# A hybrid attention and mLSTM layer: terms of the later modulation sums begin with the fifth iteration of the attention loop in place of the first

## The chip, the cores and the metric

The kernel runs on one core of one Trainium2 chip. The metric is the device time of one execution in microseconds (us). Engines are named as in the profile: PE is TensorE, DVE VectorE, ACT ScalarE, POOL GpSimd, and SP the SyncE queue that issues nearly all DMAs.

## The reference

One layer on 1024 latent tokens and 256 context tokens, all of width 1024, in float32. The parts that matter here:

```python
mod = jax.nn.silu(c) @ w_mod[l] + b_mod[l]                     # 1024 -> 6 * 1024
sh1, sc1, g1, sh2, sc2, g2 = jnp.split(mod, 6, axis=-1)
h = modulate(rms_norm(x, norm1_w[l]), sh1, sc1)
aq, ak, av, mq, mk, mv, mo, mg, ga, gm = split_in_proj(h @ w_in[l])
att = windowed_gqa(q, k, v, k_ctx, v_ctx, attn_sink[l])        # 16 heads, 4 groups, window 128
ml = mlstm_readout(ht, mo, ml_norm_w[l])                       # two mLSTM scans
y = merge_branches(att, ml, ga, gm, w_branch_att[l], w_branch_ml[l], w_out[l])
x_mid = x + g1[:, None, :] * y
x = x_mid + g2[:, None, :] * conv_ffn(modulate(rms_norm(x_mid, norm2_w[l]), sh2, sc2), ...)
```

The first two sixths of `mod` (sh1, sc1) are needed before anything else. The other four (g1, sh2, sc2, g2) are needed only behind the two mixers. They are "the later modulation sums" of the title.

## The kernel before, in words

Every float32 operand of a large product is split into a high part of fewer bits and the rest (`split_from`, L49: a copy on ACT, L44, and a subtraction on DVE), and three products are made of the pairs (`mm3`, L96 to L98). Weights come by DMA through two raw buffers (`w1r`, L71) and are split likewise (ACT `w1h`, DVE `w1l`, L74).

The stages follow each other: a startup with the context's keys and values, attention, the mLSTM (it begins with gate mathematics and projections `kv`), the merge, the feed-forward part.

Attention runs over 4 head groups g and 8 blocks b of 128 tokens, 32 pairs in all, as a pipeline of 37 iterations n. Iteration n makes the projection of pair n (`proj`), the transposed query and key of pair n - 1 (`stacks`), the scores and the softmax of pair n - 3 (`scores`), and the products with the values of pair n - 4 (`pv`). The softmax's mask step is L625 on DVE, its exponential L629 on ACT, its scaling L638 on POOL. The block of scores `s` has one PSUM buffer for the four heads of a pair, so the scores of a head wait for the mask step of the head before it. Between these, PE is given products of a later need (`filler`, L711: the sigmoid gates' projection, weights `fr`, results `g`, stored from `fo`), 24 an iteration.

Beside that the loop makes the later modulation sums. A sum has 512 columns of `w_mod`. Its k-th term is a 128 x 512 piece of the weights times a column of silu(c), added to the running sum `macc` on DVE. The first term is `tensor_scalar` (L219) and the seven others `scalar_tensor_tensor` (L221). `mod_load` (L206) brings the next piece into `wmb`, of which there is one buffer, as there is of `macc`. Behind the eighth term `mod_row` sums over the partitions on PE (L232, `ms`), adds the bias on DVE (L234), and for the second sum stores g1. Six sums, 48 terms, belong to attention; two more are made at the end of the kernel.

The order on each engine is not the order of the code. A list scheduler under the kernel places instructions by its own model of when they are ready, code order deciding between those that are; it may move an instruction far ahead of code that stands before it. Each engine then runs its list strictly in that order, and waits on semaphores.

Of the kernel before, what the change touches and what calls it, by code (L numbers as in the profile page):

```python
# [105 lines left out]
def layer_kernel(ctx: ExitStack, tc: tile.TileContext, A: dict, out: bass.AP, dbg=None):  # L106
# [58 lines left out]
    with ExitStack() as st:  # L165
        at = attention_setup(E, st)
        stage_startup(E, at)
        if "hT" in dbg:
            for k in range(KT):
                nc.sync.dma_start(dbg["hT"][0, k * P : (k + 1) * P], hH[k].bitcast(F32))  # L170
                nc.sync.dma_start(dbg["hT"][1, k * P : (k + 1) * P], hL[k].bitcast(F32))
        if dbg.get("stop") != "hT":
            stage_attention(E, st, at)
# [35 lines left out]
def mod_product(E, pool, n, last):  # L209


    nc, (i, k) = E.nc, divmod(n, KT)
    q, o = i // 2, i % 2 * 4
    if k == 0:
        E.macc = pool.tile([P, 512], F32, tag="macc", name=f"macc{i}", bufs=1)
        E.maccs[i] = E.macc
    w = E.wmod
    if k == 0:
        nc.vector.tensor_scalar(E.macc, w, E.sil[:, 0:1], None, op0=ALU.mult)  # L219
    else:  # L220
        nc.vector.scalar_tensor_tensor(E.macc, w, E.sil[:, k : k + 1], E.macc, op0=ALU.mult, op1=ALU.add)  # L221
    if k == KT - 1:
        mod_row(E, pool, i)
    if n + 1 < last:
        mod_load(E, pool, n + 1)
# [295 lines left out]
def stage_attention(E, st, at):  # L521
# [55 lines left out]
    def stacks(g, b):  # L577
        n = f"{g}_{b}"
        qf, ss = S1.pop((g, b))
        kf = wp.tile([P, 2, HD], F32, tag="kf", name=f"kf{n}", bufs=2)  # L580
        nc.vector.tensor_scalar(kf, qf[:, None, 256:320].to_broadcast([P, 2, HD]), ss[:, 4:5], None, op0=ALU.mult)


        pt = tp_tile(f"qt{n}")
        for i in range(2):
            nc.tensor.transpose(pt[:, i * P : (i + 1) * P], qf[:, i * P : (i + 1) * P], ident)
        nc.tensor.transpose(pt[:, 256:384], kf.rearrange("p r d -> p (r d)"), ident)
        QT = wp.tile([P, 512], F32R, tag="QT", name=f"QT{n}", bufs=3)
        Q4 = QT.rearrange("p (i r t) -> p r i t", i=2, r=2)
        pq = pt[:, 0:256].rearrange("p (i t) -> p i t", i=2)  # L590
        halves = slice(0, HD), slice(HD, P)
        for r in range(2):
            hi, lo = halves[r], halves[1 - r]
            copy_act(nc, Q4[hi, r], pq[hi])
        ts = sl(b * P, P)
        copy_act(nc, G[g]["KA"][:, ts], pt[:, 256:384])
        for r in range(2):
            hi, lo = halves[r], halves[1 - r]
            nc.vector.tensor_tensor(Q4[lo, r], pq[hi], Q4[hi, r].bitcast(F32), op=ALU.subtract)
        nc.vector.tensor_tensor(G[g]["KB"][:, ts], pt[:, 256:384], G[g]["KA"][:, ts].bitcast(F32), op=ALU.subtract)  # L600
        S2[(g, b)] = (QT, ss)
# [39 lines left out]
    def pv(g, b):  # L641
        n = f"{g}_{b}"
        Ps, b0, b1 = S3.pop((g, b))
        nk = b1 - b0 + NCB
        po = mm_tile(f"po{n}")
        parts = []

        def values(kb, prior=None):
            ph, plo = parts[kb]
            v = G[g]["V"][:, b0 + kb] if kb < b1 - b0 else Vc[:, kb - (b1 - b0), g]  # L650
            with behind(prior):
                nc.tensor.matmul(po, v, ph, start=kb == 0, stop=False)
                nc.tensor.matmul(po, v, plo, start=False, stop=kb == nk - 1)

        for kb in range(nk):
            pt = tp_tile(f"pt{n}_{kb}")
            for h in range(4):
                turned = nc.tensor.transpose(pt[:, h * P : (h + 1) * P], Ps[h][:, kb * P : (kb + 1) * P], ident)  # L658
            ph = pp.tile([P, 512], F32R, tag="ph", name=f"ph{n}_{kb}", bufs=3)
            plo = pp.tile([P, 512], F32R, tag="pl", name=f"pl{n}_{kb}", bufs=3)  # L660
            split_from(nc, ph, plo, pt)
            parts.append((ph, plo))
            if kb >= 2:
                values(kb - 2)
        values(nk - 2)
        values(nk - 1, FILL.products(6))
        o2 = wp.tile([HD, 512], F32, tag="o2", name=f"o2{n}", bufs=1)
        copy_act(nc, o2, po[HD:P])
        nc.vector.tensor_tensor(o2, po[0:HD], o2, op=ALU.add)
        nc.sync.dma_start(  # L670
            attT_d[g * 256 : (g + 1) * 256, b * P : (b + 1) * P].rearrange("(h d) t -> d h t", d=HD),
            o2.rearrange("d (h t) -> d h t", h=4),
        )
# [21 lines left out]
    def filler(n):  # L695
        c, t = n // 2, n % 2
        if t == 0:
            fh = fp.tile([P, KT, P], F32R, tag="fh", name=f"fh{c}")
            fl = fp.tile([P, KT, P], F32R, tag="fl", name=f"fl{c}")
            for i in range(2):  # L700
                raw = wts.rp.tile([P, 2, 400], F32, tag="raw", name=f"fr{c}_{i}").rearrange("p a b -> p (a b)")
                raw = raw[:, :512].rearrange("p (k c) -> p k c", c=P)
                nc.sync.dma_start(raw, A["w_g"][c][:, 4 * i : 4 * i + 4, :])
                split_from(nc, fh[:, 4 * i : 4 * i + 4], fl[:, 4 * i : 4 * i + 4], raw)
            FW[c] = [(fh[:, k], fl[:, k]) for k in range(KT)]
        ps = E.fl_tile(f"g{c}_{t}")
        ts = sl(t * 512, 512)
        todo = [(w, x[:, ts]) for (wh, wl), (xh, xl) in zip(FW[c], hT) for w, x in ((wh, xh), (wh, xl), (wl, xh))]

        def one(i, w, x):  # L710
            return lambda: nc.tensor.matmul(ps, w, x, start=i == 0, stop=i == len(todo) - 1)  # L711

        FILL.todo = [one(i, w, x) for i, (w, x) in enumerate(todo)]
        FILL.tile = c, t, ps

    def filled():
        if not FILL.todo and FILL.tile is None:
            return
        FILL.products(len(FILL.todo))
        c, t, ps = FILL.tile  # L720
        FILL.tile = None
        o = fp.tile([P, 512], F32, tag="fo", name=f"fo{c}_{t}", bufs=1)
        copy_act(nc, o, ps)
        dst = (E.sga_d, E.sgm_d)[c // 8]
        nc.sync.dma_start(dst[(c % 8) * P : (c % 8 + 1) * P, t * 512 : (t + 1) * 512], o)
# [5 lines left out]
    done = 0  # L731
    mod_load(E, dp, 0)
    for n in range(N + 5):
        if n % 2 and done < 48:
            mod_product(E, dp, done, 48)
            done += 1
        if n < N:
            proj(*seq[n])
        if 0 <= n - 1 < N:
            stacks(*seq[n - 1])  # L740
        if n not in SKIPS and n < N + len(SKIPS):
            filler(n - sum(s < n for s in SKIPS))
        if 0 <= n - 3 < N:
            scores(*seq[n - 3])
        if 0 <= n - 4 < N:
            pv(*seq[n - 4])
        filled()
        if done < 48:
            mod_product(E, dp, done, 48)
            done += 1  # L750

# [1281 lines left out]
```

## Time and profile before

| what | value |
|---|---|
| time, median of 3 runs | 1908.57 us (1906.63 to 1910.79) |
| time of the profiled execution | 1906.98 us |
| span of the profiled execution, first to last instruction | 1904.9 us |
| PE busy | 1878.7 us, 99% of the span |
| DVE busy | 1439.1 us, 76% |
| ACT busy | 994.3 us, 52% |
| POOL busy | 310.6 us, 16% |
| granted PE clock, mean | 0.999 |

The lines of a profile read so: start in us from the beginning of the span, duration, engine, line of the kernel, operation, what it writes <- what it reads, and in brackets how long the engine stood before it and what ended that. Buffer numbers are left out of the names. A line can be a helper's, as L44 and L49 are, so tiles tell more than lines.

### The profile page before, as it was taken

Reading aid. Unit: us, or ns where it says so; the run is one execution under the profiler, and the core shown is the slowest. Engines: PE = TensorE matmul, PEld = TensorE weight load, DVE = VectorE, ACT = ScalarE, POOL = GpSimd, SP = SyncE. Lnnn points to the kernel's source line nnn. Section 1 sums busy time; section 2 is a strip of 40 time slices with the busy share of each in tenths; the row PEclk is TensorE's granted clock in tenths of the full one; section 3 lists DMA queues with packets and bytes.
Section 4 is the critical chain, followed back from the end, with each engine's and each line's share of the span. In section 5 each row is a group of like instructions: output and inputs, shape, how many; then the busy total and the mean of one; then the engine's idle time right before and its main releaser. Section 6 shows DMA issues by size and latency. Waiting matters only on the chain.

```text
span 1904.9 us, 28762 instructions
## 1 busy us (share of the span) xinstructions
PE 1878.7 (99%) x10021; PEld 1629.9 (86%) x10021; DVE 1439.1 (76%) x2904; ACT 994.3 (52%) x1974; POOL 310.6 (16%) x524
## 2 busy tenths in 40 slices
PE   7999999999999999999999999999999999999999
PEld 4888888988888899999998887888888888888887
DVE  3967778877677766667577878679888889897565
ACT  4735656556556445454446664276444444465441
POOL 1223424333332231212020012000000000000000
PEclk9999999999999999999999999999999999999999
DMA  9542222222122423334318963613355444489841
GB/s 365 190 135 65 68 71 74 92 67 79 59 64 84 136 85 127 126 126 166 136 54 309 378 252 136 229 67 111 143 195 194 185 163 171 171 321 352 293 166 67
DMA packets 139569, 298.53 MB, mean 157 GB/s; under 512 B 15504, under 2 KB 39968, under 8 KB 136608
## 3 DMA queue, kind: packets, MB, share of 16 engines
q1 hardware_dynamic: 125024, 270.48, 40.8%
q10 hardware_dynamic: 14400, 26.22, 4.0%
q8 instruction: 79, 1.29, 0.3%
q14 instruction: 66, 0.54, 0.1%
HBM read 220.55 MB, written 76.10 MB: 156 GB/s over the span
## 4 chain that ended last, share of the span: by engine, by line
PE 87%; DVE 6%; DMA 2%; ACT 2%; POOL 2%; issue 1%; POOLq 0%; SPq 0%; DVEq 0%; ACTq 0%
PE g L711 9%; PE pa L1610 4%; PE pa L1612 4%; PE pa L1611 4%; PE pt L658 3%; PE yb L1612 2%; PE yb L1611 2%; PE yb L1610 2%; PE kv L96 2%; PE pq L96 2%; PE kv L97 2%; PE kv L98 2%; PE pq L97 2%; PE pq L98 2%; PE dx L1610 2%; PE dx L1612 2%
## 5 line engine op out<-in xcount | busy, mean ns | idle before, releaser
L638 POOL TENSOR_SCALAR P<-P,st 128x640 f32<-128x640 f32 (+1 forms) x128 | 106.8, 852 | 222.7 <-ACT ph L44 75.9
L629 ACT ACTIVATE P<-P,st 128x640 f32<-128x640 f32 (+1 forms) x128 | 102.8, 803 | 59.1 <-DVE st L625 59.0
L625 DVE CUSTOM_DVE_ANT_0 P<-s,maskA,nsink 128x640 f32<-128x640 f32 (+1 forms) x112 | 103.0, 920 | 22.1 <-PE s L621 20.4
L49 DVE TENSOR_TENSOR pl<-pt,ph 128x512 fp32r<-128x512 f32 x152 | 100.5, 683 | 4.5 <-ACT ph L44 3.4
L44 ACT ACTIVATE ph<-pt 128x512 fp32r<-128x512 f32 x152 | 86.2, 594 | 30.4 <-PE pt L658 29.1
L711 PE MATMUL g<-hH,fh 128*128 128x512 f32 x256 | 101.3, 396 | 0.0
L711 PE MATMUL g<-hH,fl 128*128 128x512 f32 x256 | 100.7, 393 | 0.5 <-DVE fl L49 0.5
L711 PE MATMUL g<-hL,fh 128*128 128x512 f32 x256 | 100.1, 391 | 0.0
L96 PE MATMUL pq<-w1h,hH 128*128 128x384 f32 (+1 forms) x256 | 87.0, 340 | 0.0
L98 PE MATMUL pq<-w1h,hL 128*128 128x384 f32 (+1 forms) x256 | 86.9, 339 | 0.0
L658 PE MATMUL pt<-ident,P 128*128 128x128 f32 x608 | 86.4, 272 | 0.3 <-POOL P L638 0.3
L97 PE MATMUL pq<-w1l,hH 128*128 128x384 f32 (+1 forms) x256 | 86.4, 338 | 0.0
L658 PEld LDWEIGHTS pt<-ident,P 128*128 128x128 f32 x608 | 72.3, 140 | 10.1 <-POOL P L638 0.6
L96 PE MATMUL mo<-w1h,hH 128*128 128x256 f32 x256 | 72.0, 281 | 0.0
L98 PE MATMUL mo<-w1h,hL 128*128 128x256 f32 x256 | 71.8, 281 | 0.0
L97 PE MATMUL mo<-w1l,hH 128*128 128x256 f32 x256 | 71.8, 280 | 0.0
L1748 ACT ACTIVATE cv<-ua,vecT 128x1024 f32<-128x1024 f32 x22 | 27.4, 1245 | 84.0 <-DVE ua L1721 84.0
L97 PE MATMUL kv<-w1l,hH 128*128 128x384 f32 x208 | 70.2, 338 | 0.0
L96 PE MATMUL kv<-w1h,hH 128*128 128x384 f32 x208 | 70.1, 337 | 0.0
L98 PE MATMUL kv<-w1h,hL 128*128 128x384 f32 x208 | 70.0, 337 | 0.0
L1022 POOL TENSOR_SCALAR kwh<-k,gcall 128x128 fp32r<-128x128 f32 x72 | 31.3, 438 | 237.3 <-PE dC L97 188.7
L1610 PE MATMUL dx<-dwh,dfh 128*128 128x512 f32 (+1 forms) x176 | 68.3, 388 | 0.0
(603 smaller groups left out, 6407.2 us busy)
## 6 DMA issues: line engine op xcount, KB each, us to landing
ur<-in_w_up SPq DMA_DIRECT2D x22, 1024.0 KB, 5.0
wmb<-in_w_modB SPq DMA_DIRECT2D x48, 256.0 KB, 2.8
f_d<-cv SPq DMA_DIRECT2D x22, 512.0 KB, 2.6
wm<-in_w_modA SPq DMA_DIRECT2D x16, 512.0 KB, 10.2
fr<-in_w_g SPq DMA_DIRECT2D x32, 256.0 KB, 3.2
drf<-fs_d SPq DMA_DIRECT2D x15, 512.0 KB, 7.1
drw<-wt_d SPq DMA_DIRECT2D x14, 512.0 KB, 6.4
w1b<-in_w_cx SPq DMA_DIRECT2D x16, 388.0 KB, 4.0
```

Of the source, the lines that this page charges most:

```text
L49: rest = nc.vector.tensor_tensor(lo, src, hi.bitcast(F32), op=ALU.subtract)
L96: nc.tensor.matmul(ps, lh[:, ls], rh[:, rs], start=start and i == 0, stop=False)
L97: nc.tensor.matmul(ps, lh[:, ls], rl[:, rs], start=False, stop=False)
L98: nc.tensor.matmul(ps, ll[:, ls], rh[:, rs], start=False, stop=stop and i == n - 1)
L625: nc.vector.tensor_tensor_reduce(pm[:, :W], ps[:, off : off + W], mask[:, :W], scale=ss[:, h : h + 1], scalar=nsink[:, hh : hh + 1], op0=A ...
L629: nc.scalar.activation(pm[:, :W], pm[:, :W], AF.Exp, bias=st4[:, h : h + 1], scale=-1.0, accum_out=st4[:, 4 + h : 5 + h])
L638: nc.gpsimd.tensor_scalar(Ps[h][:, :W], Ps[h][:, :W], st4[:, 12 + h : 13 + h], 1.0, op0=ALU.mult, op1=ALU.mult)
L658: turned = nc.tensor.transpose(pt[:, h * P : (h + 1) * P], Ps[h][:, kb * P : (kb + 1) * P], ident)
L711: return lambda: nc.tensor.matmul(ps, w, x, start=i == 0, stop=i == len(todo) - 1)
L1610: nc.tensor.matmul(ps, lh, rh, start=start and i == 0, stop=False, skip_group_check=True)
L1611: nc.tensor.matmul(ps, lh, rl, start=False, stop=False, skip_group_check=True)
L1612: nc.tensor.matmul(ps, ll, rh, start=False, stop=stop and i == n - 1, skip_group_check=True)
```

## The change

The two places of the loop that make a term now do so from n = 4 on. The load of the very first piece stays ahead of the loop. By the code, iterations 0 to 3 made six terms (one, two, one, two), and the 48 were made by iteration 31; now they are made by iteration 35.

```diff
     done = 0
     mod_load(E, dp, 0)
     for n in range(N + 5):
-        if n % 2 and done < 48:
+        if n % 2 and n >= 4 and done < 48:
             mod_product(E, dp, done, 48)
             done += 1
         if n < N:
             proj(*seq[n])
...
         filled()
-        if done < 48:
+        if n >= 4 and done < 48:
             mod_product(E, dp, done, 48)
             done += 1
```

What the scheduler makes of it differs on PE, DVE, ACT and SP from the second projection to the gate mathematics of the mLSTM; POOL's order is the same. Three places follow.

DVE near the fourth projection (`pq_3`). `macc` is the first sum and `wmb` its pieces; `P_0_0` is the first mask step of the kernel, `gtile`, `V` and `ss` belong to the projection. Before:

```order
L581 TENSOR_SCALAR kf_2_1452<-qf_2_1342,ss_2_1337 128x128
L221 SCALAR_TENSOR_TENSOR macc_1212<-wmb_1535,sil,macc_1212 128x512
L221 SCALAR_TENSOR_TENSOR macc_1212<-wmb_1723,sil,macc_1212 128x512
L548 TENSOR_TENSOR gtile<-pq_3_1408,gb 128x16
L551 TENSOR_TENSOR V_1129<-pq_3_1408,V_1129 128x64
L625 ISA P_0_0_1478,st_0_1466<-s_0_0_1467,maskA,nsink,ss_0_1160 128x512
```

Now:

```order
L221 SCALAR_TENSOR_TENSOR macc_1703<-wmb_2061,sil,macc_1703 128x512
L221 SCALAR_TENSOR_TENSOR macc_1703<-wmb_2260,sil,macc_1703 128x512
L548 TENSOR_TENSOR gtile<-pq_3_1392,gb 128x16
L551 TENSOR_TENSOR V_1129<-pq_3_1392,V_1129 128x64
L221 SCALAR_TENSOR_TENSOR macc_1703<-wmb_2475,sil,macc_1703 128x512
L555 TENSOR_REDUCE ss_3_1422<-sq_3_1420 128x5
```

The sixth to eighth term stand here, where the seventh and eighth stood; all eight terms of the first sum are still among the first four projections. The mask step now comes behind the eighth term and the rest of the projection's steps, and on PE twenty products of the filler stand between the first and the second head's scores, where six stood.

DVE near the last projection (`pq_7`), at the tail of the loop. `o_2` is the result of a pair, `fl` the rest of the filler's weights, `w1l` that of the first weights of the mLSTM, `P_4_0` a mask step. Before:

```order
L49 TENSOR_TENSOR fl_7084<-fr_0_7085,fh_7083 128x512
L669 TENSOR_TENSOR o_2_6726<-po_2_6664,o_2_6726 64x512
L49 TENSOR_TENSOR fl_7084<-fr_1_7089,fh_7083 128x512
L74 TENSOR_TENSOR w1l_7547<-w1r_7544,w1h_7546 128x2x384
L551 TENSOR_TENSOR V_5395<-pq_7_6739,V_5395 128x64
L599 TENSOR_TENSOR QT_6_6788<-qt_6_6784,QT_6_6788 64x2x128 x2
L600 TENSOR_TENSOR KB_5394<-qt_6_6784,KA_5393 128x128
L625 ISA P_4_0_6818,st_4_6806<-s_4_0_6807,maskA,nsink,ss_4_6199 128x640
```

Now:

```order
L49 TENSOR_TENSOR fl_7068<-fr_0_7069,fh_7067 128x512
L234 SCALAR_TENSOR_TENSOR m_70<-ms_6709,vecT 128x4
L219 TENSOR_SCALAR macc_6717<-wmb_6715,sil 128x512
L669 TENSOR_TENSOR o_2_6701<-po_2_6639,o_2_6701 64x512
L49 TENSOR_TENSOR fl_7068<-fr_1_7073,fh_7067 128x512
L221 SCALAR_TENSOR_TENSOR macc_6717<-wmb_6719,sil,macc_6717 128x512
L551 TENSOR_TENSOR V_5370<-pq_7_6721,V_5370 128x64
L625 ISA P_4_0_6800,st_4_6788<-s_4_0_6789,maskA,nsink,ss_4_6174 128x640
```

The sixth sum begins here; its eight terms end between the softmax steps of the pair two later. The split of the mLSTM's first weight now follows seventeen rows behind `fl`. On SP one load of `wmb` stands just ahead of the first seven loads of the mLSTM's weights (`w1r`), five among them and one just behind, and the sixth sum's products on PE (L232) among the last products of the last pair.

ACT at the same place; `w1h` is the high part of the mLSTM's weights, `V`, `QT`, `KA` and `sq` belong to the last projections. Before:

```order
L44 ACTIVATE fh_7083<-fr_1_7089 128x512
L44 ACTIVATE w1h_7546<-w1r_7544 128x2x384
L44 ACTIVATE V_5395<-pq_7_6739 128x64
L44 ACTIVATE QT_6_6788<-qt_6_6784 64x2x128 x2
L44 ACTIVATE KA_5393<-qt_6_6784 128x128
L44 ACTIVATE w1h_7552<-w1r_7550 128x2x384
L553 ACTIVATE sq_7_6766<-pq_7_6739 128x320
L629 ACTIVATE P_4_0_6818,st_4_6806<-P_4_0_6818,st_4_6806 128x640
```

Now:

```order
L44 ACTIVATE fh_7067<-fr_1_7073 128x512
L44 ACTIVATE V_5370<-pq_7_6721 128x64
L44 ACTIVATE QT_6_6770<-qt_6_6766 64x2x128
L553 ACTIVATE sq_7_6748<-pq_7_6721 128x320
L44 ACTIVATE QT_6_6770<-qt_6_6766 64x2x128
L44 ACTIVATE KA_5368<-qt_6_6766 128x128
L44 ACTIVATE w1h_7546<-w1r_7544 128x2x384
L629 ACTIVATE P_4_0_6800,st_4_6788<-P_4_0_6800,st_4_6788 128x640
```

Two splits of weights stood ahead of the projection's square and of the exponential; now the first stands behind the square and the second behind the exponential.

## The prediction

> **What bounds the kernel now.** I read the page first, then busy time by stretch, then the waits of TensorE (PE) stretch by stretch, then the tiles of the moved work, and last the timeline around the longest waits. The page's first part and its chain of waits:
>
> ```profile
> PE 1878.7 (99%) x10021; PEld 1629.9 (86%) x10021; DVE 1439.1 (76%) x2904; ACT 994.3 (52%) x1974; POOL 310.6 (16%) x524
> ...
> PE 87%; DVE 6%; DMA 2%; ACT 2%; POOL 2%; issue 1%; POOLq 0%; SPq 0%; DVEq 0%; ACTq 0%
> ```
>
> PE is busy 99% of the span and carries 87% of the chain. The change takes no product from PE and gives it none, so only what PE waits can move. Busy time by stretch (columns: PE, weight loads, VectorE (DVE), ScalarE (ACT), GpSimd, granted clock, DMA share, GB/s); attention runs from about 95 to 640 us:
>
> ```profile
> 30.00:35.00 5.00, 4.01 (x26) 3.82 (x27) 3.49 (x12) 4.20 (x11) 0.00 (x0) 0.78 1.05 401
> ...
> 90.00:130.00 40.00, 39.02 (x199) 34.67 (x197) 22.96 (x61) 14.23 (x31) 8.04 (x12) 1.00 0.45 148
> 130.00:220.00 90.00, 88.93 (x504) 79.04 (x505) 71.24 (x188) 55.30 (x126) 34.42 (x48) 1.00 0.24 72
> 220.00:580.00 360.00, 360.00 (x2082) 322.86 (x2081) 272.58 (x697) 207.29 (x482) 125.86 (x176) 1.00 0.23 70
> 580.00:600.00 20.00, 18.51 (x108) 16.08 (x107) 14.29 (x35) 12.53 (x27) 5.25 (x8) 1.00 0.33 95
> 600.00:640.00 40.00, 39.84 (x228) 33.44 (x227) 28.73 (x62) 25.27 (x55) 11.91 (x23) 1.00 0.25 73
> ```
>
> From 220 to 580 us PE never stands. It stands 0.98 + 1.07 us before that and 1.49 + 0.16 us after it. The whole of attention therefore holds 3.7 us of idle PE, and a change inside it cannot win much more. The waits of PE, first for 90 to 220 us, then for 570 to 640, then for 640 to 700 (total us, times, longest):
>
> ```profile
> PE s L618 <- DVE st L625: 0.7, 1, 0.7
> PE g L711 <- DVE fl L49: 0.5, 1, 0.5
> PE po L652 <- ACT ph L44: 0.5, 2, 0.3
> PE pt L658 <- POOL P L638: 0.3, 1, 0.3
> ```
> ```profile
> PE s L618 <- DVE st L625: 1.1, 2, 0.6
> PE po L653 <- DVE pl L49: 0.4, 1, 0.4
> PE po L652 <- ACT ph L44: 0.2, 1, 0.2
> ```
> ```profile
> PE gTir L912 <- DVE Ic L904: 0.7, 1, 0.7
> ```
>
> **The moved work.** The tile of the running sum, its row of products, its loads, and what DVE waited for them:
>
> ```profile
> L221 DVE SCALAR_TENSOR_TENSOR macc<-wmb,sil,macc x42: 721/747/1200, 102.7 to 547.5; 128x512 f32<-128x512 f32 x42
> L219 DVE TENSOR_SCALAR macc<-wmb,sil x6: 476/624/1025, 98.9 to 513.0; 128x512 f32<-128x512 f32 x6
> L232 PE MATMUL ms<-expo,macc x48: 164/250/250, 152.4 to 598.6; 128*128 128x1 f32 x48
> DMA to landing us min/median/max: 2.6/2.8/3.8
> DVE macc L221 <- DMA wmb<-in_w_modB: 20.9, 13, 3.5
> ```
>
> There are 48 terms, six sums of eight: a first one (L219) and seven more (L221). Each is one DVE instruction and one 256 KB load. There is one load buffer, so a load is issued by SP after the term before it, and the term waits about 2.8 us for it. Thirteen of the 48 made DVE stand, 20.9 us in all, 1.6 us each.
>
> By the loop, six terms leave iterations 0 to 3 and six enter iterations 32 to 35. The order of the built program says something else. The first sum's eight terms keep their places at DVE's start (the scheduler moves them up); what moves is every later sum. Its first term waits for the products (L232) of the sum before, and these keep to the loop: the first now follow block 4 of the first head group in place of block 0, four iterations later. So the second sum leaves the stretch from 153 us on, and the sixth goes from 513 to 547 us into the tail: its first term now stands right ahead of this step, which ran at 580 us:
>
> ```profile
> 580.01 0.68 DVE L669 TENSOR_TENSOR o<-po,o 64x512 f32<-64x512 f32 x1 [0.42 <-ACT o L44]
> ```
>
> Number, duration and loads of the terms are unchanged: 7 x 0.747 + 0.624 = 5.9 us of DVE a sum.
>
> **Term 1, the start.** The wait of 0.7 us in the timeline of DVE and PE:
>
> ```profile
> 128.09 0.75 DVE L221 SCALAR_TENSOR_TENSOR macc<-wmb,sil,macc 128x512 f32<-128x512 f32 x1 [3.14 <-DMA wmb<-in_w_modB]
> ...
> 129.36 0.80 DVE L625 CUSTOM_DVE_ANT_0 P<-s,maskA,nsink 128x512 f32<-128x512 f32 x1
> ```
> ```profile
> 128.89 0.40 PE L711 MATMUL g<-hL,fh 128*128 128x512 f32 x1
> 129.12 0.40 PE L711 MATMUL g<-hH,fl 128*128 128x512 f32 x1
> 130.23 0.39 PE L618 MATMUL s<-KA,QT 128*128 128x256 f32 x1 [0.71 <-DVE st L625]
> ```
>
> DVE stood 3.14 us for a term's load; the mask step (L625) behind it came late, and PE's next scores with it. Products start 0.23 us apart (128.89, 129.12), but between 129.12 and 130.23 lie 1.11: the loss is 0.88, where the idle time says 0.71. The end of a product in the records (0.40 long) overlaps what is really lost, so I add 0.17 to each wait. The Trainium skill, Perfetto Trace Analysis, Tensor Engine Instruction, says that the profile's end of a PE instruction is computed from its size and not observed; the trace agrees (0.40 long, 0.23 apart). With idle times alone, the sum at the end would be -0.9 in place of -1.7.
>
> In the new order the scheduler puts twenty products between the first two blocks of scores, where six stood: 14 x 0.23 = 3.2 us more cover against the same kind of wait. I take the 0.9 as won. The other waits in the timeline of PE:
>
> ```profile
> 97.36 0.50 PE L711 MATMUL g<-hH,fl 128*128 128x512 f32 x1 [0.50 <-DVE fl L49]
> ...
> 177.31 0.50 PE L652 MATMUL po<-ph,V 128*128 128x512 f32 x1 [0.28 <-ACT ph L44]
> ...
> 193.23 1.20 PE L658 MATMUL pt<-ident,P 128*128 128x128 f32 x9 [0.33 <-POOL P L638]
> ...
> 194.63 0.50 PE L652 MATMUL po<-ph,V 128*128 128x512 f32 x1 [0.20 <-ACT ph L44]
> ```
>
> The one on fl, at 97 us, lies ahead of the first term (98.9) and stays. The other three (0.5 + 0.3, with 3 x 0.17 = 1.3) lie amid and behind the second sum, which leaves; but their releasers are ACT and GpSimd, so I take half, -0.65. Term 1: -1.5. Bounds: all three go, -2.2; a new wait as long as the longest of the stretch in place of the won one, +0.9.
>
> **Term 2, loads of the next stage at the tail.** The timeline of ACT, DVE and PE:
>
> ```profile
> 583.55 0.84 ACT L44 ACTIVATE w1h<-w1r 128x768 fp32r<-128x768 f32 x1 [3.05 <-DMA w1r<-in_w_ml]
> ```
> ```profile
> 584.43 0.96 DVE L74 TENSOR_TENSOR w1l<-w1r,w1h 128x768 fp32r<-128x768 f32 x1 [2.85 <-ACT w1h L44]
> ...
> 586.70 0.93 DVE L625 CUSTOM_DVE_ANT_0 P<-s,maskA,nsink 128x640 f32<-128x640 f32 x1
> ```
> ```profile
> 587.70 0.45 PE L618 MATMUL s<-KA,QT 128*128 128x384 f32 x1 [0.52 <-DVE st L625]
> ```
>
> ACT stands 3.05 us for a weight of the next stage, DVE 2.85 us behind it, and PE's scores wait for the mask. In the new order five rows of ACT stand between fl's split and this one where none stood, and seventeen of DVE, two of them terms. The two waits on L618 (1.1 + 2 x 0.17 = 1.4) I take as gone, the one on L653 (0.4 + 0.17) as half gone: -1.7. Bounds: -2.0, and 0 if the load, now issued behind one more term's load on SP, lands as late as it is now needed.
>
> **Term 3, the sixth sum in the tail.** There the loop has no projection left, so less PE work covers DVE. DVE is idle 5.71 + 11.27 = 17.0 us from 580 to 640; 5.9 us more raise it from 72% to 82%. Its loads stand on SP among the weights of the next stage and among stores that wait for ACT, and a late load holds the mask steps behind it on DVE, for which PE waits. Bounds: nothing, as from 220 to 580 us, where 32 terms cost PE none; and 8 x 0.7 = 5.6 us, the longest wait of the trace's attention for each. Nearest is 130 to 220 us, where the second sum's eight terms stood beside 1.07 us of idle PE and DVE was busy 79%. I take +1.2.
>
> **Term 4, the gates.** PE waits 0.7 us for Ic, because DVE stood for a load ahead of it:
>
> ```profile
> 645.16 0.69 DVE L1140 TENSOR_TENSOR s_ba<-s_ba,s_ba 128x512 f32<-128x512 f32 x1 [1.37 <-DMA s_ba<-in_w_ba]
> ```
>
> The sixth row of products (eight short ones) now stands at the very end of attention, in front of this, which shifts PE and gives cover; but the loads of s_ba are issued a place later on ACT, and Ic still stands behind L1140. +0.3, bounds -0.7 (the wait goes) and +1.0.
>
> Sum: -1.5 - 1.7 + 1.2 + 0.3 = **-1.7 us**. The profiled execution took 1906.98 us (span 1904.9); that gives 1905.3. The median of the runs lies 1.6 above it, so **1906.9 us**. The forecast's own bounds are -4.9 and +7.5.
>
> **The rivals.**
>
> *Slower: late loads in the tail.* Each of the eight terms makes PE wait 0.7 us: +5.6, of term 1 the sure 0.9 won, term 2 eaten up: +4.7, **1913.3 us**. For it: no projection covers DVE there, 13 of 48 terms waited for their load, and the DMA engines are busier from 580 to 600 us (0.33) than in the stretch before (0.23). Against it: from 600 to 640 PE loses 0.16 us with DVE at 72%. It decides from 0.6 us a term. Chance 0.24.
>
> *Slower through the clock.* One late load is long enough (3.5 us, the longest) for PE to stand through it and for its clock to fall; from 30 to 35 us the granted clock was 0.78 in a stretch with PE waits, 5 x 0.22 = 1.1 us lost. +3.5 + 1.1 - 1.5 = +3.1, **1911.7 us**. The Trainium skill, TensorE: Matmul & The Clock Gate, Part 1, says that an idle window of some 3.4 us halves the clock; attention's longest wait is 0.71 us, at a clock of 1.00. Chance 0.03.
>
> *The change does not do what it says.* The first eight terms keep their places, and the early waits come from something else (fl, ph, GpSimd), while the tail gives back what it wins: **1908.6 us**. Chance 0.10.
>
> *All attention's waits go.* Early 1.5 + 4 x 0.17, tail 1.7 + 4 x 0.17, in all -4.5: **1904.1 us**. For it: the early load wait and the two late weights both get more cover in the new order. Against it: ACT and GpSimd, which end the others, do not get less work. Chance 0.17.
>
> The forecast keeps 0.46. 0.2% (3.8 us, so 1904.8 and 1912.4) is about what a measurement of this kernel can tell from no change. Faster by more: 0.15 of the clean case and 0.04 of the forecast's spread, 0.19. Slower by more: 0.20 of the tail case, 0.01 of the clock's and 0.02 of the forecast's, 0.23. Within it 0.58. The range 1903.4 to 1914.0 leaves out the upper part of the tail case (0.10), the low end of the clean one (0.05) and a little of the forecast's spread (0.02).
>
> **What would show it.** Right: in the profile after, no wait of PE for L625 near 130 us; none for L625 behind a split of w1r near 587; 0 to 2 us of PE waits between 590 and 630, behind DVE waits on wmb; PE idle in attention at 2 to 3 us. Wrong: terms of the second sum before 200 us; more than 3 us of PE idle between 580 and 640; a granted clock under 1.00 there; or a time that moves while PE's idle time in attention does not.

## The result, and the profile after

| | time, median of the runs | ratio to the kernel before (95% interval) |
|---|---|---|
| before | 1909.07 us (13 runs, 1906.63 to 1911.35) | |
| changed | 1912.76 us (13 runs, 1910.82 to 1914.96) | 1.0020 (1.0011 to 1.0028) |

The changed kernel is slower by 3.7 us. Its profiled execution took 1914.31 us, with a span of 1912.2 us. The same stretches by busy time, with the columns as before (PE, weight loads, DVE, ACT, GpSimd, granted clock, DMA share, GB/s):

```profile
30.00:35.00 5.00, 3.58 (x22) 3.39 (x23) 3.79 (x12) 4.20 (x9) 0.00 (x0) 0.77 1.05 396
...
90.00:130.00 40.00, 39.50 (x207) 35.76 (x206) 22.22 (x59) 13.16 (x28) 7.25 (x12) 1.00 0.48 148
130.00:220.00 90.00, 85.93 (x479) 76.28 (x478) 64.67 (x176) 52.09 (x121) 29.88 (x44) 0.98 0.19 54
220.00:580.00 360.00, 358.26 (x2067) 321.25 (x2065) 271.12 (x692) 205.53 (x478) 126.44 (x176) 1.00 0.24 70
580.00:600.00 20.00, 20.00 (x119) 17.97 (x118) 16.54 (x40) 13.54 (x29) 6.21 (x8) 1.00 0.35 102
600.00:640.00 40.00, 39.87 (x223) 33.10 (x222) 32.72 (x70) 26.81 (x60) 10.78 (x14) 1.00 0.35 104
```

From 580 to 640 us PE now stands 0.13 us where it stood 1.65: the tail is better. But it stands 4.07 us from 130 to 220, at a granted clock of 0.98, and 1.74 us from 220 to 580, where it never stood. The waits of PE, for 90 to 220 us and for 220 to 570 us (from 570 to 640 us none is listed):

```profile
PE s L618 <- DVE st L625: 4.1, 2, 3.4
PE g L711 <- DVE fl L49: 0.5, 1, 0.5
```
```profile
PE s L618 <- DVE st L625: 1.7, 2, 1.6
```

**The first pair.** The timeline of DVE up to the first mask step of the kernel, and of PE behind it:

```profile
130.10 0.75 DVE L221 SCALAR_TENSOR_TENSOR macc<-wmb,sil,macc 128x512 f32<-128x512 f32 x1 [3.15 <-DMA wmb<-in_w_modB]
...
133.81 0.75 DVE L221 SCALAR_TENSOR_TENSOR macc<-wmb,sil,macc 128x512 f32<-128x512 f32 x1 [2.36 <-DMA wmb<-in_w_modB]
134.48 0.48 DVE L555 TENSOR_REDUCE ss<-sq 128x5 f32<-128x320 f32 x1
...
136.92 0.29 DVE L600 TENSOR_TENSOR KB<-qt,KA 128x128 fp32r<-128x128 f32 x1
137.12 0.80 DVE L625 CUSTOM_DVE_ANT_0 P<-s,maskA,nsink 128x512 f32<-128x512 f32 x1
```
```profile
134.22 0.39 PE L711 MATMUL g<-hL,fh 128*128 128x512 f32 x1
137.99 0.38 PE L618 MATMUL s<-KA,QT 128*128 128x256 f32 x1 [3.38 <-DVE st L625]
...
138.60 0.63 PE L711 MATMUL g<-hH,fl 128*128 128x512 f32 x1
139.03 0.63 PE L711 MATMUL g<-hH,fh 128*128 128x512 f32 x1
```

Two terms wait for their loads, 3.15 and 2.36 us, the projection's steps take 2.6 us (134.48 to 137.12), and only then comes the mask step. PE's twenty products are out by 134.22 + 0.23, and it stands 3.38 us. Behind that its products start 0.43 us apart (138.60, 139.03) in place of 0.23: the clock has fallen, to 0.57 of full speed from 138 to 142 us.

**The third head group's weights.** The timelines of SP, ACT, DVE and PE near 265 us:

```profile
258.06 0.33 SPq L725 DMA_DIRECT2D sga_d<-fo  x1
258.46 0.41 SPq L71 DMA_DIRECT2D w1r<-in_w_att  x1
```
```profile
263.42 0.85 ACT L44 ACTIVATE w1h<-w1r 128x768 fp32r<-128x768 f32 x1 [4.25 <-DMA w1r<-in_w_att]
```
```profile
264.30 0.96 DVE L74 TENSOR_TENSOR w1l<-w1r,w1h 128x768 fp32r<-128x768 f32 x1 [3.44 <-ACT w1h L44]
...
268.16 0.80 DVE L625 CUSTOM_DVE_ANT_0 P<-s,maskA,nsink 128x512 f32<-128x512 f32 x1
```
```profile
269.03 0.39 PE L618 MATMUL s<-KA,QT 128*128 128x256 f32 x1 [1.59 <-DVE st L625]
```

It is the pattern of the tail in the kernel before: the split of a weight that is needed much later waits for its load, and a mask step stands behind it. The load is issued at 258.46, 3.4 us ahead of the pair's first scores on PE (261.84), and used from 263.42, 5.0 us later. In the kernel before it is issued 4.3 us ahead of them (253.11 and 257.45). The same split on DVE waits there too, but starts 0.07 us ahead of those scores, and not 2.46 behind them:

```profile
257.38 0.96 DVE L74 TENSOR_TENSOR w1l<-w1r,w1h 128x768 fp32r<-128x768 f32 x1 [2.43 <-ACT w1h L44]
...
261.88 0.80 DVE L625 CUSTOM_DVE_ANT_0 P<-s,maskA,nsink 128x512 f32<-128x512 f32 x1
```

**Where the time went.** The start of the first L618 of a pair marks PE's progress. The starts of pairs 1, 2, 9, 10 and 26, and of the first `dC` product of the mLSTM, give these steps (us); "after2" is a second profiled execution of the changed kernel, told below, as are the others:

| kernel | 1 to 2 | 2 to 9 | 9 to 10 | 10 to 26 | 26 to dC | sum |
|---|---|---|---|---|---|---|
| before | 13.25 | 116.78 | 15.87 | 259.61 | 145.81 | 551.3 |
| changed | 17.25 | 115.26 | 17.75 | 260.36 | 144.69 | 555.3 |
| after2 | 15.76 | 115.27 | 17.30 | 260.48 | 145.53 | 554.3 |
| late2 | 12.10 | 115.96 | 17.34 | 260.48 | 144.48 | 550.4 |
| late8 | 12.10 | 115.68 | 17.69 | 260.62 | 144.68 | 550.8 |
| late8w | 12.11 | 115.14 | 15.70 | 260.55 | 144.33 | 547.8 |
| late8w2 | 12.10 | 115.81 | 15.73 | 260.70 | 145.06 | 549.4 |
| n1 | 13.64 | 116.08 | 16.55 | 263.79 | 145.45 | 555.5 |
| n2 | 17.14 | 115.69 | 17.21 | 261.43 | 146.18 | 557.7 |
| btail | 13.79 | 116.81 | 15.88 | 259.66 | 143.78 | 549.9 |
| btail2 | 12.10 | 118.04 | 16.07 | 259.39 | 143.62 | 549.2 |
| sum6short | 17.54 | 114.69 | 18.12 | 260.69 | 144.12 | 555.2 |
| cover | 15.82 | 115.21 | 17.10 | 261.04 | 144.47 | 553.6 |

The changed kernel loses 4.0 us at the first pair, wins 1.5 us up to the ninth, loses 1.9 there and 0.8 up to the 26th, and wins 1.1 us in the tail: 4.0 in all, 3.0 in its second execution. The medians say 3.7. The same kernel can differ by 0.7 to 0.8 us in one step between two executions (the tails of changed and after2, of late8w and late8w2), so smaller differences say little.

Not all of this is waiting. The change also moves work of PE: one row of eight short products (L232, `ms`) leaves the step from the second to the ninth pair and comes into the tail. In the changed kernel it stands at the end of attention, and 0.81 us lie from its start to that of the next product:

```profile
646.93 0.95 PE L232 MATMUL ms<-expo,macc 128*128 128x1 f32 x8
647.74 0.42 PE L96 MATMUL kv<-w1h,hH 128*128 128x384 f32 x1
```

So of the 1.5 us won up to the ninth pair 0.8 are moved work and 0.7 a real gain, and the tail gains not 1.1 but 1.9 us (1.1 in the second execution), of which the row takes 0.8 back. The total is not touched by this.

The rest of the 7.3 us between the two profiled spans lies outside these steps. The start of the first filler product differs by 1.9 us (96.13 and 98.04 us), in a startup whose order is the same, and over the thirteen profiles of this study it lies between 96.1 and 100.2 us. The other 1.4 us lie behind the first `dC` product, where the stretch to the end takes 1226.1 us before and 1227.5 now, and 1226.1 to 1228.8 over the thirteen profiles.

### The profile page after: what moved, and what is told of

It is laid out like the page before. It is cut to its first block, busy times and chain, and to the rows that moved or that the text cites. A ratio compares the mean times of both kernels' runs of the same rounds, so it can differ in the third digit from the quotient of the medians.

```text
span 1912.2 us, 28757 instructions
## 1 busy us (share of the span) xinstructions
PE 1881.8 (98%) x10021; PEld 1631.5 (85%) x10021; DVE 1439.6 (75%) x2904; ACT 994.0 (52%) x1974; POOL 310.9 (16%) x524
## 4 chain that ended last, share of the span: by engine, by line
PE 85%; DVE 7%; DMA 3%; ACT 2%; issue 1%; POOL 1%; POOLq 0%; SPq 0%; ACTq 0%; DVEq 0%
PE g L711 8%; PE pa L1610 4%; PE pa L1611 4%; PE pa L1612 4%; PE pt L658 3%; PE yb L1612 2%; PE yb L1611 2%; PE yb L1610 2%; PE dx L1612 2%; PE dx L1610 2%; PE kv L96 2%; PE dx L1611 2%; PE kv L98 2%; PE kv L97 2%; PE pb L1611 2%; PE pb L1610 2%
```

## The experiments

`tc.issue_after(ins)` (in the kernel `behind`) queues instructions behind another one of the same engine. `MASKS` and `EXPS` hold the mask steps and exponentials by head group, block and head. Unless a text says otherwise each kernel computes all that the changed one does. Each ratio is to runs of the kernel before on the same chip, whose median was 1909.05 to 1910.15 us there; between chips the ratios are compared, not the times.

**late2: the seventh and eighth term behind the first mask step.** At both places of the loop:

```diff
-            mod_product(E, dp, done, 48)
+            with behind(MASKS[(0, 0, 0)] if 6 <= done < 8 else None):
+                mod_product(E, dp, done, 48)
```

> The changed kernel, with the seventh and eighth term of the first sum queued on DVE behind the first mask step of the first pair; from the second pair on the order is the changed kernel's. Theory A (PE stands 3.4 us at the first pair's scores because its mask step stands on DVE behind these two terms, their late loads and a projection's steps, and the clock falls behind that wait): the wait for L625 near 134 us goes down to under 1 us, the granted clock stays 1.00 there, and the time falls by 3.5 to 4.5 us, to 1908.3 to 1909.3. Rival B (the time is lost later, with the sixth sum in the tail): 1912 to 1913.5. Rival C (the wait only moves to the second head's scores, since the two terms now stand between the mask steps): 1911 to 1912.

**late8: the whole first sum behind the first pair's last mask step.** The same with `MASKS[(0, 0, 3)] if 0 <= done < 8`.

> The changed kernel, with all eight terms of the first sum queued behind the last mask step of the first pair, so that the terms really begin late. Theory A: as with two terms moved, and the two load waits of 3 us ahead of it go too, which cost PE nothing; 1908.3 to 1909.3. Rival B (tail): 1912 to 1913.5. Rival C: the eight terms and their loads fall among the softmax steps of the first three pairs and cost PE there what they cost before, 1911 to 1912.

late2: 1909.96 us, ratio 0.9997 (0.9989 to 1.0006). late8: 1908.29 us, 0.9988 (0.9979 to 0.9997). Both are back at the kernel before or ahead of it, and the step from the first pair to the second fell from 17.25 to 12.10 us. In late8 the waits of PE from 90 to 220 us, and its mask step, which now follows the projection's first steps at once, are:

```profile
PE s L618 <- DVE st L625: 0.8, 2, 0.4
PE g L711 <- DVE fl L49: 0.3, 1, 0.3
```
```profile
130.59 0.23 DVE L551 TENSOR_TENSOR V<-pq,V 128x64 fp32r<-128x64 f32 x1 [0.29 <-ACT V L44]
130.93 0.81 DVE L625 CUSTOM_DVE_ANT_0 P<-s,maskA,nsink 128x512 f32<-128x512 f32 x1
```

So theory A holds: the loss stood at the first pair, in the first sum's terms, not in the tail. By the ratios the fall is 4.4 us (1.0020 to 0.9997) and 6.1 us (to 0.9988), where 3.5 to 4.5 were expected; by the sums of the steps it is 4.9 and 4.5. Rival C is in part true: in late2 a wait of 0.9 us came up in the second pair. In both kernels the scheduler again put six products between the first two heads' scores.

**n1, n2: other starts.** `n >= 1` and `n >= 2` in place of `n >= 4`.

> Terms begin with the second iteration in place of the fifth. The order of DVE and PE at the first pair is that of the kernel before (six products of the filler between the first two heads' scores, the mask step behind the eighth term). Theory A: no long wait there, PE idle near 130 us about 0.7 us, time within 1 us of the kernel before: 1908 to 1910. Rival B (the later the sums end, the longer): 1909.3 to 1909.8, which cannot be told from that.

> Terms begin with the third iteration. The sums end in iteration 33, two iterations ahead of the changed kernel, but at the first pair the order is that of the changed kernel (twenty products between the first two heads' scores, the mask step behind the eighth term and a projection's steps). Theory A: the 3.4 us wait at the first pair is there, with the fall of the clock: 1911.5 to 1913.5, though only two iterations are given up. Rival B (the tail): a third to a half of the loss at most, 1909.5 to 1911.

n2: 1915.82 us, 1.0029 (1.0018 to 1.0041), with the wait at the first pair (3.27 us) and the fall of the clock, as theory A says. The time itself lies above the expected range: n2's steps add up to 2.4 us more than the changed kernel's, behind the tenth pair, where its order is another one too. Moving the start by two iterations costs at least as much as moving it by four, and the step at the first pair is the same (17.14 and 17.25 us): the loss there hangs on the order at the first pair, not on how late the sums end. n1: 1912.25 us, 1.0014 (1.0005 to 1.0023), a miss for both theories. Its step at the first pair is nearly that of the kernel before (13.64 us), but it loses 4.2 us between the 10th and the 26th pair. One of its four waits from 220 to 580 us:

```profile
455.16 0.75 DVE L221 SCALAR_TENSOR_TENSOR macc<-wmb,sil,macc 128x512 f32<-128x512 f32 x1 [2.01 <-DMA wmb<-in_w_modB]
...
458.47 0.94 DVE L625 CUSTOM_DVE_ANT_0 P<-s,maskA,nsink 128x640 f32<-128x640 f32 x1
```
```profile
459.47 0.44 PE L618 MATMUL s<-KA,QT 128*128 128x384 f32 x1 [1.25 <-DVE st L625]
```

A term waits for its load ahead of a projection's steps and a mask step: the same shape as at the first pair, in a stretch where PE in the kernel before never stands.

**late8w: the third head group's split moved too.** late8, and `w1h` and `w1l` of those weights queued behind the ninth pair's first mask step and exponential:

```diff
         if b == 0:
+            if g == 2:
+                wts.behind = MASKS[(1, 0, 0)], EXPS[(1, 0, 0)]
...
+        with ExitStack() as queued:
+            for ins in self.behind:
+                queued.enter_context(self.tc.issue_after(ins.ins))
+            self.last = copy_act(nc, h, raw)
+            self.rest = nc.vector.tensor_tensor(lo, raw, h.bitcast(F32), op=ALU.subtract)
+        self.behind = ()
```

> The run with the first sum behind the first pair (late8, 1908.3 us), and beside it the split of the first weights of the third head group (w1h on ACT, w1l on DVE) queued behind the exponential and the mask step of the first head of the ninth pair, where it stood ahead of them and waited for its load. Theory A (the wait of 1.5 us near 263 us comes from this split's late load): the wait goes, nothing takes its place, and the time falls by 1.2 to 1.8 us, to 1906.5 to 1907.1. Rival: the load is late whatever stands behind it, and the next heads' mask steps wait in place of the first: 1908 to 1908.6.

1907.03 us, 0.9992 (0.9983 to 1.0001); in a second set of runs of the same kernel, late8w2, 1906.15 us, 0.9986 (0.9978 to 0.9995).

> The run with both repairs of the changed kernel (late8w) once more, as the fastest so far. By its trace PE loses in attention 3.1 us less than in the kernel before: 0.998 to 0.999 of the time of the kernel before, and 5 to 6 us below the changed kernel on the same chip.

The step at the ninth pair went from 17.69 to 15.70 us (15.73 in late8w2), that of the kernel before, and ACT splits the weights right behind the exponential, without a wait (line numbers are 7 higher here):

```profile
259.52 0.72 ACT L636 ACTIVATE P<-P,st 128x512 f32<-128x512 f32 x1
...
260.24 0.83 ACT L44 ACTIVATE w1h<-w1r 128x768 fp32r<-128x768 f32 x1
```

So the wait came from the late load ahead of the mask step, and nothing took its place at this pair. In the time this second move is not shown: late8 had the ratio 0.9988, and 0.9992 and 0.9986 cannot be told from it, where 1.2 to 1.8 us were expected. Both moves together beat the changed kernel by 6.6 us of median on the same chip (1906.15 and 1912.70).

**btail, btail2: the tail of the kernel before.** In the kernel before the first two splits of the mLSTM's weights are queued behind mask steps and exponentials of the fourth last pair; btail2 also has late2's edit.

```diff
+            if h == 0 and k2 in {0: (3, 4, 0), 1: (3, 4, 1)}:
+                wts.behind = E.masks[...], E.exps[...]
             if h == 0 or k2 < KT // 2 - 1:
```

> The kernel before, with the splits of the first two weights of the mLSTM queued behind the mask step and the exponential of the first and the second head of the fourth last pair. Theory A (these splits and their late loads cause the waits of PE at 587 to 593 us in the kernel before): those waits of 1.5 us idle time, 2.1 with what the records hide, go, and the time falls by 1.5 to 2.1 us, to 1908.0 to 1908.6 beside 1910.1 for the kernel before on this chip. Rival (the splits are needed there by the mLSTM's first products, or PE then waits behind 600 us): no change, 1909.6 to 1910.6.

> The kernel before with both repairs: the two splits of the mLSTM's weights queued as in btail, and the seventh and eighth term of the first sum queued behind the first mask step. Theory A: 2.1 us at the tail and up to 0.9 us at the first pair, 1907.1 to 1908.4. Rival: the two terms among the mask steps cost at the second pair what they no longer cost at the first (1.2 us of waits near 146 us in late2), so 1908.0 to 1909.

btail: 1908.07 us, 0.9992 (0.9983 to 1.0001). The waits on L618 and L653 there are gone, and the step from the 26th pair on fell from 145.81 to 143.78 us, where 1.5 to 2.1 us were expected; the median fell by only 1.2 us (from 1909.28 on that chip), and the ratio's interval just includes no change. btail2: 1907.75 us, 0.9990 (0.9982 to 0.9999), inside its expectation and its rival's. The steps decide for the rival: the first fell from 13.79 us in btail to 12.10, and the second rose from 116.81 to 118.04, with a new wait of PE of 0.95 us on L618 in the second pair. The two terms cost there most of what they no longer cost at the first.

**sum6short: less work in the tail.** The changed kernel without seven terms and seven loads of the sixth sum:

```diff
-    else:
+    elif i != 5:
         nc.vector.scalar_tensor_tensor(E.macc, w, E.sil[:, k : k + 1], E.macc, ...)
...
-    if n + 1 < last:
+    if n + 1 < last and not 40 <= n < 47:
```

> The changed kernel, with the sixth sum cut to its first term: seven terms (5.2 us of DVE) and seven loads are left out of the tail, the row of products stays. Without them the first splits of the mLSTM's weights stand again ahead of the fourth last pair's softmax. Theory of the prediction's third term (the terms cost PE 1.2 us in the tail): 1911.5, down by 1 to 1.5 us beside the changed kernel's 1912.8. Theory A (the terms cost nothing, and hold the splits back): no gain, or a loss of up to 2 us, with a wait of PE for L625 behind a split of w1r near 590 us again: 1912.5 to 1914.5.

1913.29 us, 1.0020 (1.0011 to 1.0029): no gain. The tail took 144.12 us, 0.6 and 1.4 us less than in the two profiles of the changed kernel (144.69, 145.53). But late2, late8, late8w, late8w2 and cover make all terms in the tail too and took 144.33 to 145.06, so the terms' cost there is 0.2 to 1.4 us and not clear of the spread. Theory A's second half fell. ACT waits 2.90 us for the first split of the mLSTM's weights, as in the kernel before, and PE does not wait for the mask step behind it:

```profile
590.90 0.84 ACT L44 ACTIVATE w1h<-w1r 128x768 fp32r<-128x768 f32 x1 [2.90 <-DMA w1r<-in_w_ml]
```
```profile
594.05 0.93 DVE L625 CUSTOM_DVE_ANT_0 P<-s,maskA,nsink 128x640 f32<-128x640 f32 x1
```
```profile
595.41 0.34 PE L618 MATMUL s<-KA,QT 128*128 128x384 f32 x1
```

Its load was issued 4.2 us ahead of that pair's first scores (587.31 and 591.54), where in the kernel before it was 3.3 (579.83 and 583.14). So the mask step comes 2.5 us behind the first scores in place of 3.6 (594.05 - 591.54; 586.70 - 583.14), which PE's other products cover.

**cover, after2: what the clock costs.** 14 useless products on PE where the long wait stands, and the changed kernel once more beside it:

```diff
-            prior = FILL.products(6) if h in (0, 1, 2) else None
+            prior = FILL.products(20 if (g, b, h) == (0, 0, 0) else 6) if h in (0, 1, 2) else None
+            if (g, b, h) == (0, 0, 0):
+                prior = cover(prior, 14)
```

> The changed kernel, with 14 useless products of 128x512 (into a PSUM tile that nobody reads) on PE at the place of the long wait, between the twentieth product of the filler and the second head's scores; DVE's order up to that place is the changed kernel's. They take 14 x 0.23 = 3.2 us at full clock, about the wait itself. Theory (the lost clock is a part of the loss of its own, 1.2 us, and comes from PE standing, not from DVE): the mask step comes at the same time, the idle time falls from 3.4 to under 0.6 us, the granted clock stays 1.00 from 138 to 142 us, and the time falls by about 1.0 to 1.4 us beside the changed kernel, though PE does 3.2 us more work. Rival (the slow products behind the wait come from something else): the clock is 0.57 there again and the time the same or longer.

> The changed kernel once more, on the same chip as cover and late8w2: 1911.5 to 1914, with the wait of 3.4 us at the first pair and the clock of 0.57 behind it; only the start of the span may differ by 1 to 2 us between executions.

cover: 1912.85 us, 1.0021 (1.0012 to 1.0030). after2: 1912.70 us, 1.0018 (1.0009 to 1.0027). PE's idle time at that place went from 3.27 us in after2 to 0.21, as expected, and the 3.2 us of useless work did not lengthen the step (15.82 beside 15.76 us); but no gain is seen. The windows 134 to 138 and 138 to 142 us say why for the profiled executions; the first fence is the changed kernel as profiled first, the second after2, the third cover:

```profile
134.00:138.00 4.00, 0.62 (x4) 0.20 (x2) 3.94 (x14) 0.03 (x1) 2.38 (x4) 1.00 0.21 66
138.00:142.00 4.00, 4.00 (x15) 3.61 (x16) 1.21 (x4) 2.20 (x5) 0.00 (x0) 0.57 0.00 0
```
```profile
134.00:138.00 4.00, 1.05 (x5) 0.55 (x3) 3.79 (x12) 0.12 (x1) 2.38 (x4) 1.00 0.20 66
138.00:142.00 4.00, 3.68 (x22) 3.21 (x23) 2.10 (x7) 2.51 (x6) 0.00 (x0) 1.00 0.00 0
```
```profile
134.00:138.00 4.00, 3.79 (x19) 2.94 (x18) 3.32 (x13) 0.79 (x2) 2.40 (x4) 1.00 0.20 66
138.00:142.00 4.00, 4.00 (x25) 3.58 (x25) 3.17 (x7) 3.07 (x8) 0.00 (x0) 1.00 0.17 16
```

In after2 PE stood 3.27 us and the clock did not fall. So the fall, worth 1.5 us (17.25 against 15.76), comes in some executions of the changed kernel and not in others. How often is told by the mean granted clock of each run, which is 0.998 in the profiled execution with the fall and 0.999 in the one without. Of the 24 runs of the changed kernel 13 have 0.998 or less, with a mean time of 1913.6 us, and 11 have 0.999 or more, with 1911.9. In cover 2 of 11 runs have 0.998 or less, in the kernel before on that chip 2 of 27. These counts are estimates, since a fall elsewhere, in the startup say (0.77 from 30 to 35 us above), lowers the mean too. By them cover does keep the clock up, as the theory says. But with 4 falls in the 11 runs of after2 only some 0.5 us (an estimate, 4/11 of 1.5) were to be won on average, and the intervals, 0.0009 to each side, cannot show that. The expected gain of 1.0 to 1.4 us was a miss: it took one execution for all.

## Why the prediction was wrong

The forecast was 1906.9 us, a gain of 1.7; measured is a loss of 3.7. The range held the time, but the likeliest case did not come, and neither did the slower rival at its place.

- **Term 1, the failed step**: "14 x 0.23 = 3.2 us more cover against the same kind of wait. I take the 0.9 as won." The cover came. But the change moved the mask step as well, behind the eighth term and the rest of the projection's steps, and the order of the change shows this in the same rows: it is not the same wait. Against the first scores of the pair the mask step ran at 1.95 us before (129.36 and 127.41) and at 7.79 now (137.12 and 129.33): 5.8 us later, with 3.2 us more cover, so 2.6 us lost. The step from pair 1 to 2 says 2.5 with the clock at 1.00 and 4.0 with its fall. The bound of +0.9 took the longest wait seen in place of adding up what now stands ahead of the mask step: from rows of the kernel before, one load wait of up to 3.5 us and some 2.6 us of projection steps (130.33 to 132.98). As worded, one wait of 0.9 in place of another, that bound would even have been 0. Why the scheduler put twenty products there is not shown directly; late2 fits that its model saw the mask step late, since with two terms moved on DVE it put six there again. More cover in its order was here the sign of a late release, not a gain in itself. The other part of the term was right in size: -0.65 was forecast for the waits amid the second sum, and 0.7 us were won from the second to the ninth pair beside the row of products that moved away.
- **The stretch from 220 to 580 us** had no term. The argument that 32 terms cost nothing there in the kernel before does not carry over to the new order: 1.4 to 1.9 us were lost at the ninth pair and 0.8 to 0.9 behind it. late8w and late8w2 show the first to be the late split of the third head group's weights. Of the second only a wait of 0.15 us (at 348 us) is seen, and its cause is open.
- **Term 2 was right.** The waits behind the mLSTM's splits are gone, and btail shows that these splits made them (2.0 us; -1.7 was forecast). Why they are gone in the changed kernel is only half settled: in sum6short the split stands ahead of the mask step again, but its load is issued 0.9 us earlier against PE.
- **Term 3 is neither borne out nor refuted.** sum6short puts the sixth sum's terms at 0.2 to 1.4 us; +1.2 was forecast, and its time shows no gain. In after2 one of them waited for its load, and PE behind it, as the rival of late loads has it, but once and not eight times (DVE, then PE):

```profile
621.46 0.75 DVE L221 SCALAR_TENSOR_TENSOR macc<-wmb,sil,macc 128x512 f32<-128x512 f32 x1 [1.63 <-DMA wmb<-in_w_modB]
622.13 0.94 DVE L625 CUSTOM_DVE_ANT_0 P<-s,maskA,nsink 128x640 f32<-128x640 f32 x1
```
```profile
623.13 0.44 PE L618 MATMUL s<-KA,QT 128*128 128x384 f32 x1 [1.06 <-DVE st L625]
```

- **Term 4**: PE's wait for `Ic` is gone, the lower bound (-0.7) and not the +0.3 taken. sum6short, without seven of the sixth sum's terms, has no such wait either, so it is not these terms that took it away. The tail as a whole (terms 2 to 4, -0.2 forecast) came out at -1.1 to -1.9 us without the row that moved into it.
- **The rivals.** The rival of the clock had the right mechanism and nearly the price (3.5 us of standing, then 1.1 us of slow products; 3.4 and 1.5 were measured) at the wrong place, the tail; it came at the first pair, where I had put a gain. "The first eight terms keep their places" was not quite true, and not harmless: the eighth now stands behind two steps of the projection, and its wait and its own time (2.36 + 0.75 us) are half of the 5.8 us by which the mask step came later.

What stays open: why the scheduler's orders for other starts put terms ahead of mask steps elsewhere (n1), where the 0.8 us behind the tenth pair go, and what the sixth sum's terms cost in the tail.

## What to carry to other kernels

When a scheduler's order changes, follow the instruction that releases the busy engine and add up what now stands ahead of it on its own engine, late loads included, before counting what the busy engine has to do meanwhile. On an engine that runs strictly in order, work that nobody needs soon and that may wait for a load belongs behind the steps that others wait for: the moves of late2, late8w and btail, of terms or of weight splits, each took away the wait that they were made for. Only the first is clear in the time too, and moved terms can cost part of the gain at the next steps (late2, btail2). A stretch without waits is no evidence for the same work in another order. And before a stretch is said to have gained, count whether the busy engine still has the same work in it.

## What the runs showed of the hardware

The clock fell behind idle times of PE of 3.27 us (n2, to 0.57 from 138 to 142 us), 3.38 (changed, 0.57) and 3.67 (sum6short, 0.63), and not behind 3.27 (after2) or 1.96 us (sum6short at 269 us); the waits of n2 and after2, n2's window, and those of sum6short:

```profile
136.96 0.38 PE L618 MATMUL s<-KA,QT 128*128 128x256 f32 x1 [3.27 <-DVE st L625]
```
```profile
138.32 0.39 PE L618 MATMUL s<-KA,QT 128*128 128x256 f32 x1 [3.27 <-DVE st L625]
```
```profile
138.00:142.00 4.00, 4.00 (x17) 3.79 (x16) 1.37 (x4) 2.30 (x6) 0.00 (x0) 0.57 0.18 66
```
```profile
138.00:142.00 4.00, 3.62 (x14) 3.22 (x15) 1.34 (x5) 2.23 (x5) 0.00 (x0) 0.63 0.00 0
...
270.00:274.00 4.00, 4.00 (x25) 3.20 (x24) 3.90 (x9) 3.18 (x7) 0.00 (x0) 1.00 0.00 0
```

Over all runs of the three kernels with such a wait (changed, n2, sum6short) 26 of 41 have a mean granted clock of 0.998 or less, where of the 88 runs of the kernel before that stand beside the experiments 9 have. So a wait of this length is on the edge: it brings the fall in some executions and not in others.

The Trainium skill, TensorE: Matmul & The Clock Gate, Part 1, has the clock halve after an idle window of about 3.4 us, and the window running freely, so that the number of slow products at a kernel's start differs from run to run. The traces agree, for a wait in the middle of a kernel too: behind the fall products start 0.43 us apart in place of 0.23, and of the two waits of 3.27 us one has the fall and one has not.
